# Silu on ScalarE in the FFN, and long-lived tiles in one SBUF tile: a two-layer SSD and HGRN2 trunk on one core

## The chip, the core and the metric

The kernel runs on one core of one Trainium2 chip. A core has a matrix engine (TensorE, PE in the profile; PEld is its weight load), three vector-like engines (VectorE, DVE; ScalarE, ACT; GpSimd, POOL) and SyncE (SP), whose queue issues all transfers of this kernel. The metric is the device time of one execution in microseconds. Each engine works through its own instructions in order and waits on semaphores for the others.

## The reference

One inference step of a small encoder for a prompt of 1024 frames and a running stream of 32 frames, in float32. Two layers: a Mamba-2 SSD mixer and then an HGRN2 mixer, each followed by a SwiGLU FFN, with RMS norms before them and one at the end. The part that the first half of the change touches is

```
def swiglu(h, w_gate, w_up, w_down):
    return (jax.nn.silu(h @ w_gate) * (h @ w_up)) @ w_down
...
x = x + swiglu(rmsnorm(x, ffn_norm_w[layer]), ffn_w_gate[layer], ffn_w_up[layer], ffn_w_down[layer])
```

with D_MODEL 1024 and a hidden width of 2816. The mixers keep running states (SSD: 32 heads of 64 x 128; HGRN2: 8 heads of 128 x 128), which are outputs too, as is the last part of the convolution's input.

## The kernel before

The frames lie along the free dimension, the features along the 128 partitions: the residual x is 8 tiles `acc` for each of two halves, of 512 and of 544 frames (512 of the prompt and the 32 of the stream). Every float32 product is made of three float32r products: an operand is split into a high part (a ScalarE Copy that rounds) and a low part (a VectorE subtraction), and TensorE adds high x high, low x high and high x low (`product`, L275; lines 282 to 284).

The FFN's hidden width is cut into 11 slabs of 256. The first slabs of a half (two of half 0, one of half 1) are the head: `ffn_up` (L995) makes gate and up products tile by tile, and runs between the last pieces of the mixer. The other slabs go through `ffn_unit` (L921), a seven-product scheme (Strassen-Winograd) on 2 x 2 blocks: a unit makes 256 output features of gate or of up from one 1024 x 256 slab of weights, in seven `part`s of 12 matmuls each (L917 to 919). Its weights are loaded by `unit_raw` (L873) as two tiles of 1024 columns, and `unit_weights` (L888) makes the seven combinations from them on VectorE (with a scratch tile `s1`) and splits each (`hl`) into one of the six `ws` buffers. `unit_raw` counts units in `NU`: an odd unit loads both its tiles into `Y`, which has one buffer; an even one takes two of the three buffers of the ring `raw`. Units come in pairs, a gate unit and then an up unit, so before the change the gate units are the odd ones.

A unit is a generator with five steps (one `part` in the first, two in the second and the third, one in the fourth and the fifth). `in_turn` (L957) lays the units over each other: up[1], gate[4], up[2], gate[5], then up[3], next gate[1], up[4], next gate[2], up[5], next gate[3], and so on. At the end of a gate unit stands its `after` (L978): tanh on ScalarE, then (tanh + 1) x gate by a scalar_tensor_tensor on VectorE; the factor 0.5 comes in `ffn_upper` (L986), where gate is multiplied by up and the result is split into `fh` and `fl`. Down products of the group of slabs before (`ffn_outs`, L1039; four weight tiles through the ring `raw`, split by `wsplit`) run at the end of the first gate unit of a group, that is after gate[5] and before up[3]; a group has two slabs, in some places one. After the second group's, `x_stat` (L832) takes the next norm's statistics (`rkeep`: squares, a Ln and an Exp on ScalarE).

Tiles come from pools: a tile of a tag waits until one of the tag's buffers is free (counts in `BUFS`, L43). Their addresses in SBUF, those of the PSUM banks, and the order in which each engine issues are worked out by a planner before the launch, from the order as written, the priorities (`lifted`) and its own estimate of times; tiles of different tags may share addresses at different times. `small` (L72) gives 128-column scratch tiles of tag `s`, five buffers for all of their uses. The SSD states `Sst` and the HGRN2 states `Sh` share the four tiles of tag `st`.

Of the kernel before, what the change touches and what calls it, by code (L numbers as in the profile page):

```python
# [16 lines left out]
P = 128  # L17
# [24 lines left out]
TW = 552  # L42
BUFS = {"xn": 16, "x": 12, "ys": 8, "cb": 4, "xd": 2, "ec": 1, "ss": 1, "xr": 2, "n": 4, "w": 3, "s": 5}  # L43
WIDTH = {k: 512 if k == "xr" else TW if k in ("x", "w") else LEN[1] for k in BUFS}


@with_exitstack
def trunk_kernel(ctx, tc, x_prompt, x_sample, state_ssd, cache_conv, state_hgrn,
# [22 lines left out]

    def small(s, w=P, dt=F32):  # L72
        return sp.tile([P, w], dt, tag="s", bufs=BUFS["s"], name=nm(s))

# [40 lines left out]

    ident = cp.tile([P, P], F32, name="ident")
    make_identity(nc, ident)
    ones = cp.tile([P, P], F32, name="ones")
    V.memset(ones, 1.0)
    epsc = cp.tile([P, 1], F32, name="epsc")  # L120
    V.memset(epsc, EPS)
    lss = cp.tile([P, 13], F32, name="lss")
    epst = lss[:, 12:13]
    mhalf = cp.tile([P, 8], F32, name="mhalf")
    G.memset(mhalf, -0.5)
    cmask = cp.tile([P, P], F32, name="cmask")
# [4 lines left out]
    rmask = cp.tile([P, LEN[1]], F32, name="rmask")  # L131
    V.memset(rmask, 1.0)
# [3 lines left out]
    for i in range(2):  # L136
        t = cp.tile([P, P], F32, name=f"scz{i}")
        V.memset(t, 0.0)
        scz.append(t)


    acc = [[cp.tile([P, LEN[h]], F32, name=f"acc{h}_{m}") for m in range(KD)] for h in range(2)]

    xss = cp.tile([P, 2, 9], F32, name="xss")
    xr = cp.tile([P, 9], F32, name="xr")

# [36 lines left out]

    vc = cp.tile([P, NVC], F32, name="vc")
    cw = cp.tile([P, 96], F32, name="cw")
    cc = cp.tile([P, 72], F32, name="cc")
    dtb = cp.tile([P, 1], F32, name="dtb")
    acol = cp.tile([P, 1], F32, name="acol")
    dcol = cp.tile([P, 16], F32, name="dcol")
    lbt = cp.tile([P, 6, 8], F32, name="lbt")  # L190
    c1, c0, nc1 = lbt[:, 3, :], lbt[:, 4, :], lbt[:, 5, :]
# [68 lines left out]
    def wraw(parts, kt):  # L260
        raw = wp.tile([P, 1024], F32, tag="raw", bufs=3, name=nm("raw"))
        r3 = raw.rearrange("p (k c) -> p k c", k=kt)
        for (lo, hi, src) in parts:
            dma(r3[:, :, lo:hi], src.rearrange("(k p) c -> p k c", p=P))
        return raw

    @lifted("wl")
    def wsplit(raw, kt):
        wh = wp.tile([P, 1024], F32R, tag="ws", bufs=6, name=nm("wh"))
        wl = wp.tile([P, 1024], F32R, tag="ws", bufs=6, name=nm("wl"))  # L270
# [32 lines left out]

    XN = ["xn"] * 16
    XN2 = ["x"] * 12 + ["cb"] * 4
# [15 lines left out]
    @lifted("norm")  # L321
    def norm(h, wc, out, tags, blocks=None, r=None):

        for (b0, bn) in blocks or ((0, LEN[h]),):
            mmb = BLK[h] if blocks is None else [(0, bn)]
            if r is None:
                r = rstd_of([acc[h][m][:, b0:b0 + bn] for m in range(KD)], mmb, 1.0 / D, bn)
            for m in range(KD):
                xf = T("n", "xf")
                stt(xf[:, :bn], acc[h][m][:, b0:b0 + bn], vc[:, wc + m:wc + m + 1], r[:, :bn], MUL, MUL)  # L330
                if m == len(out):
                    out.append((T(tags[2 * m], "h", F32R), T(tags[2 * m + 1], "l", F32R)))
# [9 lines left out]

    carry = cp.tile([P, NCT, 3], F32, name="carry")
    newc = cp.tile([P, 2, 3, NCT], F32, name="newc")
    Sst = [cp.tile([P, 512], F32, tag="st", bufs=NG, name=f"Sst{g}") for g in range(NG)]
    cumd = [dp.tile([32, LEN[h]], F32, name=f"cumd{h}") for h in range(2)]
# [4 lines left out]
    def ssd_dt(h, xn, blocks):  # L351
# [33 lines left out]
        act(pk[96:128, :L], cum[96:128, :L], AF.Exp)  # L385
        lastc = cp.tile([P, 5], F32, name=f"lastc{h}")
        V.tensor_copy(lastc[96:128, :4], pk[96:128, P - 1:H1:P])
# [4 lines left out]
        dma(lastd[h][:, :nch], lastc[96:128, :nch])  # L392
        elast = cp.tile([P, 32, 5], F32, tag="elast", bufs=2, name=f"elast{h}")
        dma(elast[:, :, :nch], lastd[h][:, :nch].unsqueeze(0).to_broadcast([P, 32, nch]))
        return pk, None, elast

    def ssd_cols(h):
        pk, _, elast = dts[h]
        cols = cp.tile([P, 5, P], F32, tag="cols", bufs=1, name=f"cols{h}")
# [174 lines left out]
    def ssd_layer(after, w0):  # L574
# [16 lines left out]
        for i, (h, g) in enumerate(units):  # L591
# [14 lines left out]
            if g == 0:  # L606
                ssd_cols(h)
            Yt = sp.tile([P, 4 * LEN[1]], F32, tag="Y", bufs=1, name=nm("Y"))
            u["Y"] = Yt.rearrange("p (j t) -> p j t", j=4)
            Ss = None  # L610
            if h:
                Ss = T("ss", "Ss")[:, :512]
                sr = T("xr", "sr")
                dma(sr.rearrange("p (j n) -> p j n", n=P),
# [33 lines left out]

    Shb = [cp.tile([P, 512], F32, tag="st", bufs=NG, name=f"Sh{i}") for i in range(2)]
    Sh = [Shb[e // 4][:, (e % 4) * P:(e % 4 + 1) * P] for e in range(8)]  # L650
# [136 lines left out]
    def hgrn_layer(after):  # L787
# [4 lines left out]
        for i, (h, e) in enumerate(units):  # L792
# [16 lines left out]
            if e % 2 == 0:  # L809
                yt = sp.tile([P, 4 * LEN[1]], F32R, tag="Y", bufs=1, name=nm("hy"))  # L810
                yp = yt.rearrange("p (j t) -> p j t", j=4)
# [19 lines left out]

    def x_stat(h, tag):  # L832

        keep = T(tag, "rkeep")
        return rstd_of([acc[h][m][:, :LEN[h]] for m in range(KD)], BLK[h], 1.0 / D, LEN[h], keep)

    def norm_pieces(h, wc, out, blocks, r):

        def piece(m, b0, bn):
            xf = T("n", "xf")  # L840
            stt(xf[:, :bn], acc[h][m][:, b0:b0 + bn], vc[:, wc + m:wc + m + 1], r[:, b0:b0 + bn], MUL, MUL)
            if m == len(out):
                out.append((T("xn", "h", F32R), T("xn", "l", F32R)))
            xh, xl = out[m]
# [28 lines left out]
    def unit_raw(src):  # L873

        NU[0] += 1
        if NU[0] % 2:
            t = sp.tile([P, 4 * LEN[1]], F32, tag="Y", bufs=1, name=nm("raw2"))
            halves = [t[:, q * 1024:(q + 1) * 1024] for q in range(2)]
        else:
            halves = [wp.tile([P, 1024], F32, tag="raw", bufs=3, name=nm("raw")) for _ in range(2)]  # L880
        out = []
# [6 lines left out]
    def unit_weights(src):  # L888
# [3 lines left out]
        def hl(x):  # L892
            w = wp.tile([P, 1024], F32R, tag="ws", bufs=6, name=nm("wh"))
# [81 lines left out]
    def ffn_gate(layer, h, s, xn, tx, g):  # L975
        L = LEN[h]

        def after(dst):  # L978
            g.extend(dst)
            for x in g:  # L980
                t = T("w", "ft")
                act(t[:, :L], x[:, :L], AF.Tanh, scale=0.5)
                stt(x[:, :L], t[:, :L], 1.0, x[:, :L], ADD, MUL)
        return ffn_unit(h, ffn_w_gate[layer][:, s * 256:(s + 1) * 256], xn, tx, "w", after)

    def ffn_upper(layer, h, s, xn, tx, g, hid):  # L986
        L = LEN[h]

        def after(dst):
            for x, y in zip(g, dst):  # L990
                stt(y[:, :L], x[:, :L], 0.5, y[:, :L], MUL, MUL)
                hid.append(split(y[:, :L], L, (T("ys", "fh", F32R), T("ys", "fl", F32R))))
        return ffn_unit(h, ffn_w_up[layer][:, s * 256:(s + 1) * 256], xn, tx, "xd", after)

    def ffn_up(layer, h, s, i, hid, xn):  # L995
# [6 lines left out]
        for (b0, bn) in BLK[h]:  # L1002
# [99 lines left out]
    def mixer_ffn(mixer, layer, wc, nxt):  # L1102
# [15 lines left out]
        r = []  # L1118
        due = ffn_half(layer, 1, xn[1], tx[1], 1, lambda: r.append(nxt and x_stat(0, "ss")),
                       [2] if nxt else [1, 1])  # L1120
# [70 lines left out]
    for q in range(2):  # L1191
        wrow.append(T(("ec", "ss")[q], "wrow")[:, :512])
        dma(wrow[q], final_norm_w[q * 512:(q + 1) * 512].unsqueeze(0).to_broadcast([P, 512]))
# [38 lines left out]
```

## Time and profile before

| | |
|---|---|
| time, median of 3 runs | 2942.97 us (2942.57 to 2947.24) |
| profiled execution, its own time | 2942.06 us |
| its span (first to last instruction) | 2940.3 us |
| mean granted TensorE clock | 0.994 |
| moved from and to HBM | 272.39 MB read, 7.82 MB written |

The profile is of one execution. Busy time is the time in which an engine had an instruction in work; matmuls are pipelined, and their ends are modelled, so that a busy TensorE isn't TensorE at its peak. Rows of groups give an engine, an operation, out<-in with the program's names, how many, and then the busy time in us and the mean of one in ns, and behind a bar the engine's idle time just before them and what ended most of it. Rows of waits give who waited for whom, the total in us, how often, and the longest. Because most helpers make their instructions on one line (L86 for ScalarE, L89 and L92 for VectorE, L98 for transfers), groups are told apart by the names of the tiles: `ft` is the FFN's tanh, `fw` the gate, `fxd` up and then the hidden value, `wh` and `wl` the split weights, `raw` any weight tile as loaded.

### The profile page before, as it was taken

The numbers are of one execution on the slowest core, as the hardware profiler recorded it, in microseconds if no ns is written. First come the engines' busy times: TensorE is split into PE (matmuls) and PEld (weight loads), VectorE is DVE, ScalarE is ACT, GpSimd is POOL, SyncE is SP. The second block draws the span as 40 slices with busy tenths as digits, with TensorE's granted clock in tenths as the row PEclk, the third lists the DMA queues.
The fourth block names the chain that finished last, engine by engine and source line by source line (L and its number), as shares of the span: only waits on it lengthen the run. The fifth ranks groups of instructions, "written<-read, shape, count | busy, mean of one in ns | idle before, by whom it ended". The sixth has DMA issues, their size and how long they took to land.

```text
span 2940.3 us, 49353 instructions
## 1 busy us (share of the span) xinstructions
PE 2855.9 (97%) x19655; PEld 2618.4 (89%) x19655; DVE 2205.6 (75%) x3879; ACT 1551.3 (53%) x2944; POOL 52.7 (2%) x156
## 2 busy tenths in 40 slices
PE   7999999999999999999999999999999999999998
PEld 6777788989988999899999888899988999999997
DVE  6877787877887987897777555655578977887777
ACT  6745545554643654455544555655554644454445
POOL 0000001000100000000000000000000000000000
PEclk9999999999999999999999999999999999999999
DMA  5443424343333333322333222222222333323332
GB/s 146 123 111 94 108 76 122 106 113 98 109 80 105 98 98 108 108 80 87 101 94 99 79 79 80 69 76 76 78 84 87 108 96 99 111 87 94 94 94 103
DMA packets 401346, 283.42 MB, mean 96 GB/s; under 512 B 28873, under 2 KB 386778, under 8 KB 401114
## 3 DMA queue, kind: packets, MB, share of 16 engines
q1 hardware_dynamic: 401114, 280.25, 32.7%
q8 instruction: 154, 2.52, 0.4%
q14 instruction: 78, 0.64, 0.1%
HBM read 272.39 MB, written 7.82 MB: 95 GB/s over the span
## 4 chain that ended last, share of the span: by engine, by line
PE 75%; DVE 12%; DMA 6%; ACT 5%; issue 2%; SPq 0%; DVEq 0%; POOL 0%; ACTq 0%; POOLq 0%
PE mm L282 16%; PE mm L284 16%; PE mm L283 16%; PE mm L919 3%; PE mm L917 3%; PE mm L918 3%; PE sc L919 3%; PE sc L917 3%; PE sc L918 3%; DMA cumB<-cumd 3%; DMA raw<-in_ffn_w_gate_dram 2%; DVE wh L89 2%; ACT wh L86 1%; PE sc L509 1%; ACT cumB L86 1%
## 5 line engine op out<-in xcount | busy, mean ns | idle before, releaser
L86 ACT ACTIVATE wh<-raw 128x512 fp32r<-128x512 f32 (+1 forms) x688 | 554.2, 817 | 592.4 <-PE mm L283 363.3
L282 PE MATMUL mm<-h,wh 128*128 128x272 f32 (+2 forms) x2064 | 675.0, 328 | 7.9 <-ACT h L86 3.9
L284 PE MATMUL mm<-h,wl 128*128 128x272 f32 (+2 forms) x2064 | 668.5, 324 | 2.7 <-DVE wl L89 2.7
L283 PE MATMUL mm<-l,wh 128*128 128x272 f32 (+2 forms) x2064 | 668.3, 324 | 1.3 <-DVE l L89 0.9
L89 DVE TENSOR_TENSOR wl<-raw,wh 128x1024 fp32r<-128x1024 f32 x308 | 376.0, 1222 | 150.7 <-ACT wh L86 149.3
L282 PEld LDWEIGHTS mm<-h,wh 128*128 128x128 f32 x2064 | 390.0, 189 | 38.1 <-ACT h L86 4.9
L284 PEld LDWEIGHTS mm<-h,wl 128*128 128x128 f32 x2064 | 390.2, 189 | 33.0 <-DVE wl L89 3.9
L283 PEld LDWEIGHTS mm<-l,wh 128*128 128x128 f32 x2064 | 390.4, 189 | 30.9 <-DVE l L89 3.1
L282 PE MATMUL mm<-fh,wh 128*128 128x272 f32 (+1 forms) x1056 | 343.2, 326 | 8.9 <-DVE fxd L89 7.8
L283 PE MATMUL mm<-fl,wh 128*128 128x272 f32 (+1 forms) x1056 | 342.2, 325 | 1.8 <-DVE fl L89 1.8
L89 DVE TENSOR_TENSOR acc<-mm,acc 128x272 f32<-128x272 f32 (+1 forms) x512 | 259.6, 524 | 110.3 <-PE mm L284 107.6
L284 PE MATMUL mm<-fh,wl 128*128 128x272 f32 (+1 forms) x1056 | 341.1, 324 | 0.6 <-DVE wl L89 0.6
L89 DVE TENSOR_TENSOR wh<-raw,wh 128x512 fp32r<-128x512 f32 x380 | 258.2, 688 | 20.6 <-ACT wh L86 17.7
L917 PE MATMUL mm<-th,wh 128*128 128x272 f32 (+1 forms) x912 | 260.9, 286 | 0.4 <-ACT s L86 0.4
L919 PE MATMUL mm<-th,wh 128*128 128x272 f32 (+1 forms) x912 | 259.6, 285 | 0.2 <-DVE wh L89 0.2
L918 PE MATMUL mm<-tl,wh 128*128 128x272 f32 (+1 forms) x912 | 259.6, 285 | 0.0
L282 PEld LDWEIGHTS mm<-fh,wh 128*128 128x128 f32 x1056 | 198.8, 189 | 26.9 <-DVE fxd L89 9.3
L283 PEld LDWEIGHTS mm<-fl,wh 128*128 128x128 f32 x1056 | 199.6, 189 | 17.7 <-DVE fl L89 3.4
L284 PEld LDWEIGHTS mm<-fh,wl 128*128 128x128 f32 x1056 | 199.5, 189 | 16.1 <-DVE wl L89 1.0
L917 PE MATMUL sc<-h,wh 128*128 128x272 f32 (+1 forms) x608 | 173.7, 286 | 0.5 <-ACT wh L86 0.5
L917 PEld LDWEIGHTS mm<-th,wh 128*128 128x128 f32 x912 | 171.7, 188 | 2.5 <-ACT s L86 1.7
L919 PE MATMUL sc<-h,wh 128*128 128x272 f32 (+1 forms) x608 | 173.3, 285 | 0.0
(261 smaller groups left out, 5961.0 us busy)
## 6 DMA issues: line engine op xcount, KB each, us to landing
raw<-in_ffn_w_down_dram SPq DMA_DIRECT2D x90, 512.0 KB, 3.5
raw<-in_ffn_w_gate_dram SPq DMA_DIRECT2D x88, 512.0 KB, 4.9
raw<-in_ffn_w_up_dram SPq DMA_DIRECT2D x88, 512.0 KB, 3.8
raw<-in_ssd_in_w_dram SPq DMA_DIRECT2D x80, 512.0 KB, 4.6
raw<-in_hgrn_in_w_dram SPq DMA_DIRECT2D x64, 512.0 KB, 4.1
cumB<-cumd SPq DMA_DIRECT2D x64, 256.0 KB, 4.1
raw<-in_ssd_out_w_dram SPq DMA_DIRECT2D x32, 512.0 KB, 3.7
raw<-in_hgrn_out_w_dram SPq DMA_DIRECT2D x16, 512.0 KB, 3.2
```

The source lines that it names most:

```text
L86: A.activation(out=out, in_=in_, func=f, **kw)
L89: (eng or V).tensor_tensor(out=out, in0=a, in1=b, op=op)
L282: PE.matmul(ps[:, :bn], a, mh, start=(k == 0), stop=False)
L283: PE.matmul(ps[:, :bn], a, ml, start=False, stop=False)
L284: PE.matmul(ps[:, :bn], b, mh, start=False, stop=(k == n - 1))
L509: PE.matmul(pp, Btok[:n, :], xw[:n, :], start=True, stop=True)
L917: PE.matmul(ps[:, :n], a, mh, start=(k == 0 and not more), stop=False, skip_group_check=True)
L918: PE.matmul(ps[:, :n], a, ml, start=False, stop=False, skip_group_check=True)
L919: PE.matmul(ps[:, :n], b, mh, start=False, stop=(k == 3), skip_group_check=True)
```

## The change

Two things. In the FFN, silu is made by ScalarE's Silu, in place on the gate tile (in the head from PSUM into `ft`), and the product with up is a plain tensor_tensor. And tiles that live long, or whose rotation is simple, are laid into one tile `fixed` of 14368 columns by `place` (which rounds each up to 16 columns), or, for the normed input, into one tile `xn` of 16 slots; what stays in pools has widths of TW (552) columns or two or four times that. The small scratch tiles become rings written out by hand. `s1` and the kept statistics move into the four `st` tiles, and `NU` is raised in `unit_weights`, after `unit_raw` has read it.

```diff
+FIXED = 14368
-BUFS = {"xn": 16, "x": 12, "ys": 8, "cb": 4, "xd": 2, "ec": 1, "ss": 1, "xr": 2, "n": 4, "w": 3, "s": 5}
-WIDTH = {k: 512 if k == "xr" else TW if k in ("x", "w") else LEN[1] for k in BUFS}
+BUFS = {"x": 12, "ys": 8, "cb": 4, "xd": 2, "ec": 1, "ss": 1, "xr": 2, "n": 4, "w": 3}
+WIDTH = {k: TW for k in BUFS}
...
-    def small(s, w=P, dt=F32):
-        return sp.tile([P, w], dt, tag="s", bufs=BUFS["s"], name=nm(s))
+    def slot(tag, s):
+        return T(tag, s, F32R) if isinstance(tag, str) else tag
+
+    rings = {"diag": (0, 2), "cbm": (2, 2), "Btok": (4, 2), "hT": (0, 2), "hSp": (2, 4), "fss": (4, 2), "nco": (0, 1)}
+    at = {}
+
+    def small(s, w=P):
+
+        at[s] = at.get(s, -1) + 1
+        if s == "hec":
+            return hec[at[s] % 3][:, :w]
+        first, n = rings[s]
+        return smalls[first + at[s] % n][:, :w]
...
+    fixed = cp.tile([P, FIXED], F32, name="fixed")
+    used = [0]
+
+    def place(w):
+        used[0] += -(-w // 16) * 16
+        return fixed[:, used[0] - -(-w // 16) * 16:][:, :w]
+
+    smalls, hec = [place(P) for _ in range(6)], [place(16) for _ in range(3)]
...
-    acc = [[cp.tile([P, LEN[h]], F32, name=f"acc{h}_{m}") for m in range(KD)] for h in range(2)]
+    acc = [[place(LEN[h]) for m in range(KD)] for h in range(2)]
...
-        raw = wp.tile([P, 1024], F32, tag="raw", bufs=3, name=nm("raw"))
+        raw = wp.tile([P, 2 * TW], F32, tag="raw", bufs=3, name=nm("raw"))[:, :1024]
...
-    XN = ["xn"] * 16
+    colt = place(5 * P)
+    xnt = cp.tile([P, 16, LEN[1]], F32R, name="xn")
+    XN = [xnt[:, i] for i in range(16)]
...
-    Sst = [cp.tile([P, 512], F32, tag="st", bufs=NG, name=f"Sst{g}") for g in range(NG)]
+    st = [place(TW) for _ in range(NG)]
+    Sst = [t[:, :512] for t in st]
...
     def unit_raw(src):
 
-        NU[0] += 1
         if NU[0] % 2:
-            t = sp.tile([P, 4 * LEN[1]], F32, tag="Y", bufs=1, name=nm("raw2"))
+            t = sp.tile([P, 4 * TW], F32, tag="Y", bufs=1, name=nm("raw2"))
...
-        s1 = T("xr", "s1")[:, :512].rearrange("p (k c) -> p k c", k=4)
+        NU[0] += 1
+        s1 = st[NU[0] % 2][:, :512].rearrange("p (k c) -> p k c", k=4)
...
             for x in g:
-                t = T("w", "ft")
-                act(t[:, :L], x[:, :L], AF.Tanh, scale=0.5)
-                stt(x[:, :L], t[:, :L], 1.0, x[:, :L], ADD, MUL)
+                act(x[:, :L], x[:, :L], AF.Silu)
...
             for x, y in zip(g, dst):
-                stt(y[:, :L], x[:, :L], 0.5, y[:, :L], MUL, MUL)
+                tt(y[:, :L], x[:, :L], y[:, :L], MUL)
...
             t = T("w", "ft")
-            act(t[:, :bn], pg[:, :bn], AF.Tanh, scale=0.5)
-            stt(t[:, :bn], t[:, :bn], 1.0, pg[:, :bn], ADD, MUL)
-            stt(t[:, :bn], t[:, :bn], 0.5, pu[:, :bn], MUL, MUL)
+            act(t[:, :bn], pg[:, :bn], AF.Silu)
+            tt(t[:, :bn], t[:, :bn], pu[:, :bn], MUL)
...
-        due = ffn_half(layer, 0, xn[0], tx[0], HEAD, lambda: r.append(x_stat(1, "ec")), [2])
+        due = ffn_half(layer, 0, xn[0], tx[0], HEAD, lambda: r.append(x_stat(1, st[2])), [2])
```

The other vectors, masks and states (`ident`, `vc`, `carry`, `lastc`, `elast` and so on) go through `place` in the same way, and the rows of the last norm's weight (`wrow`) lie in `st[2]` and `st[3]`.

More of the change, by code (lines that the diff above doesn't have):

```diff
@@ L130, in trunk_kernel @@
     umask = cmask.bitcast(U32)
-    rmask = cp.tile([P, LEN[1]], F32, name="rmask")
+    rmask = place(LEN[1])
     V.memset(rmask, 1.0)
@@ L136, in trunk_kernel @@
     for i in range(2):
-        t = cp.tile([P, P], F32, name=f"scz{i}")
+        t = place(P)
         V.memset(t, 0.0)
         scz.append(t)
-    acc = [[cp.tile([P, LEN[h]], F32, name=f"acc{h}_{m}") for m in range(KD)] for h in range(2)]
-    xss = cp.tile([P, 2, 9], F32, name="xss")
-    xr = cp.tile([P, 9], F32, name="xr")
+    acc = [[place(LEN[h]) for m in range(KD)] for h in range(2)]
+    xss = place(2 * 9).rearrange("p (a b) -> p a b", b=9)
+    xr = place(9)
     def x_rows(h, c):
@@ L182, in over_partitions @@
             PE.matmul(out[:, c * P:c * P + n], ones[:n, :], d[:n, :n], start=True, stop=True)
[L184 to L190, printed above, removed]
+    vc = place(NVC)
+    cw = place(96)
+    cc = place(72)
+    dtb = place(1)
+    acol = place(1)
+    dcol = place(16)
+    lbt = place(6 * 8).rearrange("p (a b) -> p a b", b=8)
     c1, c0, nc1 = lbt[:, 3, :], lbt[:, 4, :], lbt[:, 5, :]
@@ L268, in wsplit @@
     def wsplit(raw, kt):
-        wh = wp.tile([P, 1024], F32R, tag="ws", bufs=6, name=nm("wh"))
-        wl = wp.tile([P, 1024], F32R, tag="ws", bufs=6, name=nm("wl"))
+        wh = wp.tile([P, 2 * TW], F32R, tag="ws", bufs=6, name=nm("wh"))[:, :1024]
+        wl = wp.tile([P, 2 * TW], F32R, tag="ws", bufs=6, name=nm("wl"))[:, :1024]
         act(wh, raw, AF.Copy)
@@ L331, in norm @@
                 if m == len(out):
-                    out.append((T(tags[2 * m], "h", F32R), T(tags[2 * m + 1], "l", F32R)))
+                    out.append((slot(tags[2 * m], "h"), slot(tags[2 * m + 1], "l")))
                 xh, xl = out[m]
@@ L385, in ssd_dt @@
         act(pk[96:128, :L], cum[96:128, :L], AF.Exp)
-        lastc = cp.tile([P, 5], F32, name=f"lastc{h}")
+        lastc = place(5)
         V.tensor_copy(lastc[96:128, :4], pk[96:128, P - 1:H1:P])
@@ L392, in ssd_dt @@
         dma(lastd[h][:, :nch], lastc[96:128, :nch])
-        elast = cp.tile([P, 32, 5], F32, tag="elast", bufs=2, name=f"elast{h}")
+        elast = place(160).rearrange("p (h c) -> p h c", c=5)
         dma(elast[:, :, :nch], lastd[h][:, :nch].unsqueeze(0).to_broadcast([P, 32, nch]))
@@ L398, in ssd_cols @@
         pk, _, elast = dts[h]
-        cols = cp.tile([P, 5, P], F32, tag="cols", bufs=1, name=f"cols{h}")
+        cols = colt[:, :5 * P].rearrange("p (c t) -> p c t", t=P)
         for c, (o, n, _) in enumerate(CHUNKS[h]):
@@ L607, in ssd_layer @@
                 ssd_cols(h)
-            Yt = sp.tile([P, 4 * LEN[1]], F32, tag="Y", bufs=1, name=nm("Y"))
+            Yt = sp.tile([P, 4 * TW], F32, tag="Y", bufs=1, name=nm("Y"))[:, :4 * LEN[1]]
             u["Y"] = Yt.rearrange("p (j t) -> p j t", j=4)
@@ L646, in half_two_dt @@
         dts[1] = ssd_dt(1, xns[1], BLK[1])
-    Shb = [cp.tile([P, 512], F32, tag="st", bufs=NG, name=f"Sh{i}") for i in range(2)]
+    Shb = [t[:, :512] for t in st[:2]]
     Sh = [Shb[e // 4][:, (e % 4) * P:(e % 4 + 1) * P] for e in range(8)]
@@ L809, in hgrn_layer @@
             if e % 2 == 0:
-                yt = sp.tile([P, 4 * LEN[1]], F32R, tag="Y", bufs=1, name=nm("hy"))
+                yt = sp.tile([P, 4 * TW], F32R, tag="Y", bufs=1, name=nm("hy"))[:, :4 * LEN[1]]
                 yp = yt.rearrange("p (j t) -> p j t", j=4)
@@ L830, in trunk_kernel, with x_stat @@
     NB = 1
-    def x_stat(h, tag):
-        keep = T(tag, "rkeep")
+    def x_stat(h, keep):
         return rstd_of([acc[h][m][:, :LEN[h]] for m in range(KD)], BLK[h], 1.0 / D, LEN[h], keep)
@@ L842, in piece @@
             if m == len(out):
-                out.append((T("xn", "h", F32R), T("xn", "l", F32R)))
+                out.append((XN[2 * m], XN[2 * m + 1]))
             xh, xl = out[m]
@@ L873, in unit_raw @@
     def unit_raw(src):
-        NU[0] += 1
         if NU[0] % 2:
-            t = sp.tile([P, 4 * LEN[1]], F32, tag="Y", bufs=1, name=nm("raw2"))
+            t = sp.tile([P, 4 * TW], F32, tag="Y", bufs=1, name=nm("raw2"))
             halves = [t[:, q * 1024:(q + 1) * 1024] for q in range(2)]
         else:
-            halves = [wp.tile([P, 1024], F32, tag="raw", bufs=3, name=nm("raw")) for _ in range(2)]
+            halves = [wp.tile([P, 2 * TW], F32, tag="raw", bufs=3, name=nm("raw"))[:, :1024] for _ in range(2)]
         out = []
@@ L892, in hl @@
         def hl(x):
-            w = wp.tile([P, 1024], F32R, tag="ws", bufs=6, name=nm("wh"))
+            w = wp.tile([P, 2 * TW], F32R, tag="ws", bufs=6, name=nm("wh"))[:, :1024]
             v = w.rearrange("p (q k c) -> p q k c", q=2, k=4)
@@ L1118, in mixer_ffn @@
         r = []
-        due = ffn_half(layer, 1, xn[1], tx[1], 1, lambda: r.append(nxt and x_stat(0, "ss")),
+        due = ffn_half(layer, 1, xn[1], tx[1], 1, lambda: r.append(nxt and x_stat(0, st[3])),
                        [2] if nxt else [1, 1])
```

20 lines of the change are left out of this document (10 added, 10 removed).

## The prediction

> **What bounds the kernel now.** I read the page first (busy time, then the chain that ended last), then stretches of each stage, then who waits for whom.
>
> ```profile
> span 2940.3 us, 49353 instructions
> PE 2855.9 (97%) x19655; PEld 2618.4 (89%) x19655; DVE 2205.6 (75%) x3879; ACT 1551.3 (53%) x2944; POOL 52.7 (2%) x156
> PE 75%; DVE 12%; DMA 6%; ACT 5%; issue 2%; SPq 0%; DVEq 0%; POOL 0%; ACTq 0%; POOLq 0%
> PE mm L282 16%; PE mm L284 16%; PE mm L283 16%; PE mm L919 3%; PE mm L917 3%; PE mm L918 3%; PE sc L919 3%; PE sc L917 3%; PE sc L918 3%; DMA cumB<-cumd 3%; DMA raw<-in_ffn_w_gate_dram 2%; DVE wh L89 2%; ACT wh L86 1%; PE sc L509 1%; ACT cumB L86 1%
> ...
> 240.00:300.00 60.00, 56.59 (x281) 44.89 (x279) 39.65 (x57) 24.66 (x46) 2.33 (x8) 1.00 0.39 110
> 1320.00:1380.00 60.00, 57.90 (x446) 57.19 (x445) 46.52 (x82) 33.08 (x60) 0.00 (x0) 0.97 0.27 81
> 1380.00:1440.00 60.00, 60.00 (x480) 59.81 (x479) 45.69 (x81) 27.53 (x52) 0.00 (x0) 1.00 0.33 105
> 1680.00:1740.00 60.00, 60.00 (x290) 48.65 (x289) 33.22 (x63) 33.21 (x52) 0.00 (x0) 1.00 0.27 79
> ```
>
> A row of a stretch is: its length, then busy time of PE, PEld, DVE, ACT and POOL, the granted clock, the DMA share and GB/s. TensorE is the bound. It is busy 2855.9 of 2940.3 us, so everything else together leaves it 84.4 us of idle time, 2.9%: no edit off TensorE can win more than that and the clock lost after such waits. The FFN (about 960 to 1620 us and 2240 to 2900 us; 1380 to 1440 is a full stretch of it) runs at 60.00 of 60 while VectorE is at 46 and ScalarE at 28 of 60. The Silu edit takes work from VectorE in just this stage, where it has 14 us of every 60 to spare; only what makes TensorE wait counts. The chain has two transfers in it, cumB in the SSD layer (untouched here) and, in the FFN, the gate weights.
>
> Who TensorE waits for (total us, times, longest):
>
> ```profile
> PE sc L509 <- DVE xw L89: 8.9, 10, 1.4
> PE mm L282 <- DVE fxd L89: 7.8, 7, 2.1
> ...
> PE sc L748 <- ACT hkv L86: 0.9, 1, 0.9
> ```
>
> The first is inside an SSD chunk, which the change leaves as it is. The second belongs to the FFN. One of its seven, from the timelines of VectorE, SyncE's queue and TensorE, with the clock behind it:
>
> ```profile
> 1328.61 0.69 DVE L89 TENSOR_TENSOR wh<-raw,wh 128x512 fp32r<-128x512 f32 x1
> ...
> 1334.89 0.69 DVE L89 TENSOR_TENSOR s<-raw 128x512 f32<-128x512 f32 x1 [2.51 <-DMA raw<-in_ffn_w_gate_dram]
> 1335.50 0.68 DVE L89 TENSOR_TENSOR sq<-sq,sq 128x512 f32<-128x512 f32 x1
> 1336.10 0.44 DVE L89 TENSOR_TENSOR fxd<-sc,s 128x272 f32<-128x272 f32 x1
> ...
> 1329.33 0.92 SPq L98 DMA_DIRECT2D raw<-in_ffn_w_gate_dram  x2
> ...
> 1336.59 0.40 PE L282 MATMUL mm<-fh,wh 128*128 128x272 f32 x1 [2.10 <-DVE fxd L89]
> ...
> 1338.00:1341.00 3.00, 3.00 (x15) 3.00 (x14) 2.64 (x4) 1.41 (x4) 0.00 (x0) 0.50 0.26 65
> 1341.00:1344.00 3.00, 3.00 (x25) 3.00 (x25) 2.08 (x4) 1.85 (x3) 0.00 (x0) 0.96 0.33 115
> ...
> 1470.93 0.69 DVE L89 TENSOR_TENSOR s<-raw 128x512 f32<-128x512 f32 x1 [2.07 <-DMA raw<-in_ffn_w_gate_dram]
> ...
> 1472.03 0.39 PE L282 MATMUL mm<-fh,wh 128*128 128x272 f32 x1 [0.41 <-DVE fxd L89]
> ```
>
> Gate units load their weights into Y, which has one buffer. The last split that reads the old gate weights starts at 1328.61, the new load is issued at 1329.33, and VectorE stands 2.51 us in front of `s<-raw`, the sum that needs it. Queued behind it on VectorE is `fxd<-sc,s`, the read that frees the PSUM bank that the down product wants, so TensorE stands 2.10 us. A wait of 2.07 us cost TensorE only 0.41: some 1.7 us are absorbed. After the long wait the granted clock is 0.50 for 3 us: 15 matmuls start there, 25 in the next 3 us, so 10 are lost, 10 x 0.12 = 1.2 us more. This was the only stretch of those that I read where the clock fell behind such a wait.
>
> **The change part by part.**
>
> ```profile
> L86 ACT ACTIVATE ft<-fw 128x544 f32<-128x544 f32 x40 | 26.1, 653 | 0.3
> L86 ACT ACTIVATE ft<-fw 128x512 f32<-128x512 f32 x36 | 22.6, 628 | 0.4
> L92 DVE SCALAR_TENSOR_TENSOR fw<-ft,fw 128x544 f32<-128x544 f32 x40 | 28.9, 721 | 1.1
> L92 DVE SCALAR_TENSOR_TENSOR fw<-ft,fw 128x512 f32<-128x512 f32 x36 | 24.8, 688 | 0.2
> L92 DVE SCALAR_TENSOR_TENSOR fxd<-fw,fxd 128x512 f32<-128x512 f32 x36 | 24.8, 690 | 0.0
> L89 DVE TENSOR_TENSOR fl<-fxd,fh 128x512 fp32r<-128x512 f32 x36 | 24.9, 692 | 0.6
> L92 DVE SCALAR_TENSOR_TENSOR ft<-ft,mm 128x512 f32<-128x512 f32 x16 | 11.0, 686 | 11.2 <-PE mm L284 8.2 <-ACT ft L86 3.0
> L92 DVE SCALAR_TENSOR_TENSOR ft<-ft,mm 128x272 f32<-128x272 f32 x16 | 7.0, 435 | 9.4 <-ACT ft L86 4.8 <-PE mm L284 4.6
> L86 ACT ACT_TABLE_LOAD x96 | 123.2, 1283 | 17.8 <-DVE hec L687 8.2 <-DVE hlg L89 7.2 <-PEq L1219 0.8
> ```
>
> *Silu.* Gate units: 40 + 36 Tanh become as many Silu over the same elements; no Silu is in this trace, the nearest row is the Tanh that it replaces, so I take equal (0). The 76 scalar_tensor_tensor that made silu go: 28.9 + 24.8 = 53.7 us of VectorE. In the heads (`ffn_up`) half of the two groups `ft<-ft,mm` goes, (11.0 + 7.0) / 2 = 9.0 us. The product with up turns from a scalar_tensor_tensor (690 ns at 512) into a tensor_tensor (692): 0. VectorE loses 62.7 us, all beside a TensorE at 60 of 60. Value on the end: 0, bounds 0 and -3.
>
> *Table loads.* The trace has 96, each 1.28 us, in front of Ln, Exp, Tanh and Sqrt groups; FFN Tanh needs none of its own after an Exp. Silu, if it lies apart from Exp, needs one wherever the FFN's activations resume after an Exp. By ScalarE's order that is seven times: twice in each layer's head, once after each of the three statistics (`rkeep`). 7 x 1.28 = 9.0 us of ScalarE, and what hides it is that ScalarE is at 28 of 60. The nearest thing on the path is the 0.9 us that TensorE waited once for `hkv` in the HGRN head. I take +1, bounds 0 and +9. The Trainium skill, "ScalarE: Activation LUTs", section "What ACT_TABLE_LOAD costs", speaks against such a change: a switch costs about 2.66 us with its drain. By that figure the seven would be 18.6 us of ScalarE; the trace's 96 loads have 123.2 us busy and 17.8 us of idle time in front of all of them, which bears out the load and shows little of a drain.
>
> *Weights.* `NU` is now raised after `unit_raw` reads it, so its parity turns: gate units load into two of the three `raw` buffers, up units into Y. The rows of the waits on both sides:
>
> ```profile
> DVE s L89 <- DMA raw<-in_ffn_w_gate_dram: 32.8, 16, 3.5
> DVE s L89 <- DMA raw<-in_ffn_w_up_dram: 24.0, 17, 2.7
> ...
> ACT wh L86 <- DMA raw<-in_ffn_w_down_dram: 149.6, 41, 5.0
> ACT wh L86 <- DMA raw<-in_ffn_w_gate_dram: 20.4, 19, 1.9
> ...
> raw<-in_ffn_w_gate_dram SPq DMA_DIRECT2D x88, 512.0 KB, 4.9
> ```
>
> Where down products run, the up unit held two `raw` buffers, so four down tiles went through the third one by one: ScalarE's 41 waits of 3.6 us. They had cover (the six split buffers hold the next parts). Now the gate's two are free by then, down tiles use three, and the next gate load comes behind them with a whole set of down products to land in (two slabs, 544 columns: 192 matmuls at 60 / 480 = 0.125 us, 24 us). So the seven waits go: -7.8, and -1.2 of clock. What is late next: the up load into Y, which is issued when the last up unit's last split is done and is wanted three parts (36 matmuls, 36 x 0.125 = 4.5 us) later, against the 4.9 us that a gate load took to land (the last row, from the page's transfers). VectorE or ScalarE will wait in front of it some 0.3 to 2 us at each of 38 up units; queued behind `s<-raw` there is the next gate unit's `fw<-sc,s`, whose bank TensorE wants. Gate loads with no down products between had the same distance, and TensorE shows no wait at them. I take +1, bounds 0 and +19 (below).
>
> *Places.* `fixed` and `xn` hold what was in tiles of their own; the work, its order as written and the counts of x, ys, cb, n, w are the same, `xn` slots are overwritten in the same sequence, and the small rings have nine places for the five of tag `s`. Waits for memory in the trace are those of rings that stay (raw, cumB). Value 0; a changed allocation also reshuffles the order in which the planner issues, which I bound by the largest stall it could make or remove in the layers, the 8.9 us of `xw`, to either side.
>
> Sum: -7.8 - 1.2 + 0 + 1 + 1 + 0 = -7.0 us on the profiled execution, 2942.06 us (span 2940.3 and 1.8 around it): 2935.1. The median of the runs, 2942.97, is 0.9 above that execution: **2936.0**.
>
> **Rivals.**
> 1. *The stall only moves.* The gate's load now queues behind down loads that wait for splits, so VectorE stands in front of the same `s<-raw`, and +9 comes back. For it: every one of these tiles goes through SyncE's one queue in order. Against: the down products give it some 24 us, of which it needs 4.9. Time 2943 (within +-4).
> 2. *Slower: Y under the up units.* 38 turnarounds in place of the 16 that hurt. If each costs TensorE what the 16 gate waits cost it, 7.8 / 16 = 0.49 us, that is 38 x 0.49 = 18.6, with the 9.0 won and 1 of tables: 2943 - 9.0 + 1 + 18.6 = 2953.6. It decides from where the wait passes the 1.7 us that are absorbed. Against it: gate loads at that distance were late by about 1.1 us (20.4 / 19).
> 3. *More: less VectorE in front of TensorE.* If the freed 62.7 us and the new order also took half of the waits on `xw` and the few on `sq`, `wl`, `fl`: a further 10, 2926.
> 4. *Tables at every pair.* If Silu's table did not hold Copy, 38 + 16 Silu groups would load twice: 54 x 2 x 1.28 = 139 us of ScalarE, still under its idle time, with TensorE hit as above by about 0.5 each: 2943 + 27 = 2970. Against it: Copy, Square and Relu cost no load anywhere beside Tanh, Exp or Ln in this trace. The same page, section "Table sets: the hidden batching unit", says that copy, relu and identity lie in every set; by that rule this rival is out.
>
> **How the numbers follow.** Forecast 0.45 (2931 to 2940), rival 1 0.28, rival 2 0.14, rival 3 0.10, rival 4 0.03. About 0.2% (5.9 us) is what a measurement of this kernel can tell from no change: faster means below 2937.1, slower above 2948.9. Of the forecast some two thirds lie below 2937.1 (0.30), with rival 3 (0.10) and a little of rival 1 (0.02): faster 0.42. Slower: rivals 2 and 4 less their lower ends, and the reshuffle's upper end: 0.17. Same: 0.41. The range reaches from rival 3 to rival 2: 2924 to 2954; the forecast's own is 2931 to 2940.
>
> **What would show it.** After: no TensorE wait on `fxd` of 1 to 2 us where down products begin; ScalarE's waits for down weights well under 149.6; VectorE waits for gate weights near 0 and those for up weights at up to 38 places, below 1.7 us each; 103 table loads; Silu at 653 and 628 ns; VectorE near 2143 us. I am wrong if TensorE waits at the up units (rival 2), if table loads pass 110 (rival 4), or if the difference lies before 900 us or between 1620 and 2240, where only the reshuffled order could have made it.

## The result, and the profile after

| | before | after |
|---|---|---|
| time, median on the same chip | 2946.41 us (2942.57 to 2949.01, 5 runs) | 2895.88 us (2894.16 to 2896.89, 5 runs) |
| ratio, 95% interval | | 0.9831 [0.9816, 0.9845] |
| span of the profiled execution | 2940.3 us | 2894.0 us |

The changed kernel is faster by 1.7%, well below the range of the prediction. The page of the kernel after, first its span and then the busy time of the engines:

```profile
span 2894.0 us, 49037 instructions
...
PE 2843.8 (98%) x19655; PEld 2615.4 (90%) x19655; DVE 2158.1 (75%) x3787; ACT 1563.9 (54%) x2951; POOL 43.2 (1%) x156
```

The work is the same on TensorE (19655 matmuls), its idle time fell from 84.4 us to 2894.0 - 2843.8 = 50.2 us, and its busy time by 12.1 us. To see where, I take the start of the instructions that add a product to the residual (`acc<-mm,acc` before, `fixed<-mm,fixed` after, 512 in both), counted from 0, and compare the same one in both traces (after less before, us):

```
number and place in the program         before    after    difference
 80  end of the SSD layer                892.6    863.5     -29.1
256  behind the first FFN               1765.0   1728.4     -36.6
352  end of the HGRN2 layer             2250.6   2212.9     -37.7
496  end of the second FFN              2906.9   2862.5     -44.4
```

So 29 us come from the SSD layer, where not a line of the arithmetic changed, 7.5 from the first FFN and the residual around it, 6.7 from the second, 1 from HGRN2. Between the same places TensorE starts the same number of matmuls in both traces. Up to the 80th accumulation its idle time falls from 48.8 to 27.1 us and its busy time from 843.8 to 836.4; from the 80th to the 256th the idle time falls from 10.1 to 4.7, from the 352nd to the 496th from 6.9 to 2.5. The prediction had looked for everything in the FFN.

**The SSD layer.** Stretches before (length, then busy PE, PEld, DVE, ACT, POOL, clock, DMA share, GB/s; in brackets the instructions that start):

```profile
100.00:380.00 280.00, 267.25 (x1330) 208.82 (x1329) 213.35 (x312) 152.46 (x281) 12.99 (x37) 1.00 0.40 107
380.00:520.00 140.00, 132.76 (x890) 116.17 (x889) 112.45 (x173) 73.99 (x159) 10.25 (x24) 0.98 0.38 102
```

and after:

```profile
100.00:380.00 280.00, 279.60 (x1411) 220.66 (x1410) 223.84 (x327) 162.79 (x302) 10.79 (x37) 1.00 0.40 109
380.00:520.00 140.00, 135.29 (x983) 120.12 (x982) 117.01 (x188) 74.61 (x164) 6.73 (x24) 1.00 0.43 113
```

In the first stretch TensorE stood 12.75 of 280 us before and 0.40 after, at the same granted clock. What it stood for is best read in the chain of work. The chain before, in order of time, between 490 and 530 us (start, length, what; SPq is the queue of SyncE; shorter pieces left out):

```profile
492.25 0.61 PE sc L520 x8
492.88 0.37 SPq L98
493.35 4.61 DMA cumB<-cumd
498.04 0.16 ACT cumB L86
498.20 0.15 issue
498.35 1.49 ACT cumB L86 x4
499.84 0.95 ACT wh L86
500.79 0.29 ACT z L86
501.17 0.29 issue
501.45 0.69 DVE xw L89
502.15 0.14 issue
502.29 1.10 PE sc L509 x2
503.38 0.61 PE sc L520 x8
504.01 3.87 DMA cumB<-cumd
507.96 0.84 ACT cumB L86 x3
```

This is a loop, once per chunk. The product `sc<-cumB,xdt` (L520) of one chunk reads a `cumB` tile for the last time; the load of a later chunk's `cumB` goes into that same place, so SyncE's queue lets it go only then; it takes 4.61 us to land; ScalarE, which works in order, stands in front of the Relu that reads it, and behind that Relu stand a weight split and a `z` that have nothing to do with it; VectorE's `xw` comes after those, and TensorE's next product (L509) after `xw`. From one L520 to the next are 11.1 us, and of them 5 are queue and transfer. The waits in the SSD layer (100 to 900 us) say the same. Before, ScalarE and SyncE's queue:

```profile
ACT cumB L86 <- DMA cumB<-cumd: 75.4, 35, 6.2
...
SPq L98 <- DVE cumB L89: 141.4, 32, 13.4
SPq L98 <- PE sc L520: 93.6, 32, 6.1
```

After:

```profile
ACT cumB L98 <- DMA cumB<-cumd: 3.0, 8, 0.6
...
SPq L110 <- ACT cumB L98: 4.4, 3, 1.6
...
SPq L110 <- PE sc L544: 0.4, 1, 0.4
```

The queue no longer waits for the product (L544 is the old L520) nor for VectorE's last pass over `cumB`, and ScalarE's 75.4 us are 3.0. Why can the load go earlier, when the ring has four buffers as before? The built programs tell: the count of a ring orders the work, but the waits come from the addresses that the planner gave.

```
                 cumB tiles  places  of these behind  median us from a load's
                                     another cumB     issue to its first Relu
before               72         4        68               4.4
after                72        29         7               9.7
```

In the kernel after, the tile that `cumB` replaces is in 65 of 72 cases one of another tag, and one that has been done with for some time. (That all pool tiles have one width now is the likely reason; no run changed the widths alone.) The load is issued some 5 us earlier, and the loop is open: the 29 us are 0.8 us for each of the 36 chunks. It isn't more because TensorE's own work is the next bound (140.00 of 140 us between 520 and 660 after).

**The FFN.** The same views after, waits first, then the stretch from 1320 to 1380 us, which the prediction showed for the kernel before (the kernel after is some 30 us further on in its program there):

```profile
DVE fixed L101 <- DMA raw<-in_ffn_w_gate_dram: 31.8, 23, 2.7
...
ACT wh L98 <- DMA raw<-in_ffn_w_up_dram: 28.5, 33, 1.8
...
ACT wh L98 <- DMA raw<-in_ffn_w_down_dram: 8.2, 5, 2.1
```

```profile
1320.00:1380.00 60.00, 59.91 (x472) 59.09 (x471) 43.18 (x75) 34.73 (x63) 0.00 (x0) 1.00 0.32 97
```

ScalarE's 149.6 us in front of down weights are 8.2, the wait of TensorE for `fxd` is gone from the list, and 472 matmuls start where 446 did, at a clock of 1.00 for 0.97. Silu and the table loads:

```profile
L98 ACT ACT_TABLE_LOAD x103 | 132.1, 1283 | 18.3 <-DVE fixed L711 15.8 <-PEq L1239 0.8
L98 ACT ACTIVATE fw<-fw 128x544 f32<-128x544 f32 x40 | 26.3, 657 | 7.4 <-DVE fw L101 6.6
L98 ACT ACTIVATE fw<-fw 128x512 f32<-128x512 f32 x36 | 22.6, 627 | 3.9 <-DVE fw L101 3.6
```

### The profile page after: what moved, and what is told of

Same layout as the page of the kernel before. It is cut to its first block, busy times and chain, and to the rows that moved or that the text cites. A ratio compares the mean times of both kernels' runs of the same rounds, so it can differ in the third digit from the quotient of the medians.

```text
span 2894.0 us, 49037 instructions
## 1 busy us (share of the span) xinstructions
PE 2843.8 (98%) x19655; PEld 2615.4 (90%) x19655; DVE 2158.1 (75%) x3787; ACT 1563.9 (54%) x2951; POOL 43.2 (1%) x156
## 5 line engine op out<-in xcount | busy, mean ns | idle before, releaser
L303 PE MATMUL mm<-xn,wh 128*128 128x272 f32 (+2 forms) x1552 | 524.2, 338 | 1.7 <-ACT xn L98 1.3
L304 PE MATMUL mm<-xn,wh 128*128 128x272 f32 (+2 forms) x1552 | 519.0, 335 | 1.2 <-DVE xn L101 1.2
L305 PE MATMUL mm<-xn,wl 128*128 128x272 f32 (+2 forms) x1552 | 518.0, 334 | 1.2 <-DVE wl L101 1.2
L101 DVE TENSOR_TENSOR wl<-raw,wh 128x1024 fp32r<-128x1024 f32 x308 | 375.5, 1221 | 75.4 <-ACT wh L98 57.4
L101 DVE TENSOR_TENSOR fixed<-mm,fixed 128x272 f32<-128x272 f32 (+1 forms) x512 | 262.5, 523 | 194.4 <-PE mm L305 192.8
L303 PEld LDWEIGHTS mm<-xn,wh 128*128 128x128 f32 x1552 | 292.9, 189 | 32.1 <-issue 2.8
L305 PEld LDWEIGHTS mm<-xn,wl 128*128 128x128 f32 x1552 | 292.9, 189 | 31.1 <-issue 2.0
L304 PEld LDWEIGHTS mm<-xn,wh 128*128 128x128 f32 x1552 | 292.5, 188 | 29.3 <-DVE xn L101 1.7
L941 PE MATMUL sc<-xn,wh 128*128 128x272 f32 (+1 forms) x608 | 173.1, 285 | 0.0
L942 PE MATMUL sc<-xn,wh 128*128 128x272 f32 (+1 forms) x608 | 172.8, 284 | 0.0
```

Of the source, the lines that this page charges most:

```text
L101: (eng or V).tensor_tensor(out=out, in0=a, in1=b, op=op)
L303: PE.matmul(ps[:, :bn], a, mh, start=(k == 0), stop=False)
L304: PE.matmul(ps[:, :bn], a, ml, start=False, stop=False)
L305: PE.matmul(ps[:, :bn], b, mh, start=False, stop=(k == n - 1))
L941: PE.matmul(ps[:, :n], a, ml, start=False, stop=False, skip_group_check=True)
L942: PE.matmul(ps[:, :n], b, mh, start=False, stop=(k == 3), skip_group_check=True)
```

## The experiments

Two theories stood against each other for the 29 us: (A) the loop through `cumB`'s transfer, (B) the places of all the other tiles (`ec` had one place before and 14 after, `cth` one and 24, `xdt` and `xw` two each and over 20), with Silu and the weights' turn as parts of their own. All ratios are against the kernel before on the same chip. The last columns compare the 80th and the 496th accumulation of one trace with those in the trace of before, from a chip on which that kernel's median was 2946.41 us; on those of the experiments it was 2936 to 2938. The kernels that were traced more than once (after and after_again, place_only and place_only_again) differ by 0.9 and 1.6 us at the 80th and by 2.5 and 1.1 at the 496th, so two or three us in these columns say nothing.

```
run                        ratio   95% interval       at 80   at 496
silu_only                  1.0038  [1.0023, 1.0053]    +2.4    +4.0
place_only                 0.9854  [0.9839, 0.9869]   -29.8   -47.1
parity_only                0.9979  [0.997, 0.9989]     +5.3    -9.4
parity_undone              1.0019  [1.0009, 1.0028]    -2.5    -0.8
cumb_four                  0.9936  [0.992, 0.9953]     -2.5   -19.8
cumb_six                   0.9964  [0.9951, 0.9977]    +0.9   -15.1
cumb_eight                 0.9938  [0.9923, 0.9953]    -5.3   -21.8
raw_three                  0.984   [0.9825, 0.9855]   -30.3   -48.8
cumb_four_544              0.9937  [0.992, 0.9953]     +2.4   -16.8
two_rings_four             0.9856  [0.9842, 0.9871]   -27.3   -46.9
parity_undone_load_ring    0.9953  [0.9938, 0.9968]   -16.1   -12.5
after_load_ring            0.9853  [0.9838, 0.9868]   -27.0   -43.7
parity_undone_load_four    0.99    [0.9886, 0.9913]   -25.7   -31.2
after_again                0.9849  [0.9836, 0.9863]   -30.0   -46.9
place_only_again           0.9849  [0.9836, 0.9862]   -31.4   -48.2
tanh_raw_three             0.9844  [0.9831, 0.9858]   -31.4   -50.7
```

### Silu alone, and everything but Silu

`silu_only` is the kernel before with the FFN's three Silu edits of the diff; `place_only` is the kernel after with tanh and scalar_tensor_tensor put back.

> The kernel before with the three Silu edits alone; tiles and NU as before. Theory A (places: a tile may lie at any free address, so its load needn't wait for the tile of its own tag) : no gain, ratio 0.998 to 1.002, PE still waits some 17 us on L509 in the SSD layer and some 8 us on fxd in the FFN. Theory B (VectorE's relief): a third or more of the 47 us, ratio below 0.995, mostly in the FFN. 103 table loads in either.

> The changed kernel with tanh and the two scalar_tensor_tensor put back; places, widths, rings and NU as changed. Theory A: nearly the whole gain, ratio 0.982 to 0.986. Theory B: a ratio of 0.988 or more, the FFN slower than in the changed kernel by 10 us or more. 96 table loads.

Silu alone won nothing and cost 0.4%; everything but Silu has the whole gain. Where the 0.4% lies the traces don't tell: silu_only's is 2.4 us late at the end of the SSD layer, before any Silu has run, and 4.0 in the end, not much more than two traces of one kernel differ by.

### The weights' turn alone, and its undoing

```diff
-        if NU[0] % 2:
+        if not NU[0] % 2:
```

`parity_only` has this line in the kernel before (gate units load into `raw`, up units into `Y`), `parity_undone` has it in the kernel after.

> The kernel before with the parity of NU turned alone: gate units load into raw, up units into Y. Theory C (the parity takes the gate load off the turnaround of Y): the waits on fxd at the start of the down products go, -7 to -10 us, ratio 0.9965 to 0.998, all of it after 960 us. Theory A alone (the parity does nothing while three raw addresses serve all loads): within 0.2%. My recorded rival 2 (Y under the up units) would show PE waits at the up units and a ratio over 1.002.

> The changed kernel with the parity of NU as before: gate units in Y. The planner gives other addresses to it as well: 13 for the 72 cumB tiles and 3 for raw, where the changed kernel has 29 and 7 and the kernel before 4 and 3. Theory A alone: the SSD gain stays for the most part (end of the SSD layer's last accumulation 20 to 29 us earlier than before), the FFN gain shrinks. Theory C: the FFN loses its 13 us, ratio to before about 0.988. If all came from Silu or the order: ratio as changed, 0.983.

The waits of parity_only in the FFN:

```profile
ACT wh L86 <- DMA raw<-in_ffn_w_up_dram: 26.7, 32, 2.1
...
DVE s L89 <- DMA raw<-in_ffn_w_gate_dram: 21.2, 16, 2.7
ACT wh L86 <- DMA raw<-in_ffn_w_down_dram: 12.7, 11, 2.1
```

That is the FFN of the kernel after, in the kernel before: no TensorE wait for `fxd` is left, and from the 80th to the 496th accumulation 14.7 us are won, 5.3 of them given back in the SSD layer in front. parity_undone was the surprise: its weights are turned back, which has nothing to do with the SSD layer, and the gain is gone there too. Its waits in that layer:

```profile
ACT cumB L98 <- DMA cumB<-cumd: 82.5, 36, 7.5
```

In its program 58 of 72 `cumB` tiles stand again behind a `cumB` (median 4.35 us from issue to Relu), with the same widths and the same `fixed`. So `fixed`, the small rings and the equal widths don't open the loop by themselves; the places that came out of the planner do, and a one-word edit elsewhere changes them. But `ec` is back in one place too here, so this run doesn't tell (A) from (B).

### cumB in a ring of its own, raw in a ring of its own

In the kernel after, `cumB` goes by hand through a ring of 4, 6 or 8 places, or `raw` through one of 3:

```diff
+    cbr = cp.tile([P, 4, TW], F32, name="cbr")
+    cbn = [0]
+
+    def cb_slot():
+        cbn[0] += 1
+        return cbr[:, cbn[0] % 4, :512]
...
-            cb = T("cb", "cumB")[:, :512].rearrange("p (h t) -> p h t", t=P)
+            cb = cb_slot().rearrange("p (h t) -> p h t", t=P)
```

> The changed kernel with cumB in a ring of four places of its own, as tag cb nominally is. The planner then also gives raw three places (380 of 384 raw tiles follow a raw tile). Theory A1 (the SSD gain is the turnaround of cumB: with four places the load of chunk c+1 waits for the last reader of chunk c-1): the last accumulation before the SSD layer's end (the 64th) is at most 5 us earlier than before, not 28; SyncE's queue waits again some 90 us on L544 and ScalarE some 75 us on cumB; ratio 0.995 to 0.999, what is left being the FFN's. Theory A2 (the order or the small rings make the SSD gain): the 64th accumulation stays 20 us or more earlier, ratio 0.986 to 0.989.

> The same with six places of 512 columns for cumB. Theory A1: a load may run a chunk further ahead, so most of the SSD gain is back, the 64th accumulation 20 to 28 us earlier than before, ratio 0.987 to 0.991, ScalarE's waits on cumB below 25 us. Theory A2: no difference to the ring of four beyond 0.2%.

> The same with eight places. Theory A1: like six or up to 5 us better, ScalarE waits on cumB below 10 us; if six is already enough, the same within 0.2%. Theory A2: as the ring of four.

> The changed kernel with raw in a ring of three places of its own; cumB stays free (12 of 72 follow another cumB). Theory A1: the SSD layer as in the changed kernel, the 64th accumulation 25 to 30 us earlier than before. For the FFN two ways: if the parity alone made its 13 us (gate loads off Y), ratio 0.982 to 0.985; if the wider choice of places for raw did, the FFN gives back 5 us or more, ratio 0.986 to 0.988.

raw_three keeps the whole gain, so `raw`'s seven places (three before) have no part in it. With four places for `cumB` the SSD layer's gain is gone, as (A) says; but six and eight did not bring it back, which I had taken for a test of (A). cumb_eight's waits in the SSD layer:

```profile
ACT cbr L105 <- DMA cbr<-cumd: 75.0, 37, 5.6
...
SPq L117 <- PE sc L551: 84.1, 28, 5.7
```

A load still waits for the product, one four chunks back now. With a bigger ring the planner moves the Relus forward by as much: one of cumb_eight's loads is issued at 107.2 us, right behind the product that ends at 107.1, ScalarE's Relu reads it at 111.2, and its own product comes only at 179. From a Relu to the product that reads its tile the median is 20.6 us with four places, 49.4 with six and 91.5 with eight; from a load's issue to its Relu it stays at 4.3, 4.4 and 4.6. These rings are always full, and so give the transfer no time, however long they are. The three runs also gave the other tiles other places: cumb_four put `ec` back in one, so it loses what (B) needs as well; cumb_six and cumb_eight have `ec` in 18 and 14 places, `cth` in 20 and 17, and are at +0.9 and -5.3 us at the 80th accumulation all the same, which speaks against (B).

### One factor at a time

A place 544 columns wide in place of 552 (`cumb_four_544`) leaves `cumB` tight and gives the other tiles about as many places as in the kernel after (`ec` 21, `cth` 24, `xdt` 20, `xw` 17). `two_rings_four` goes the other way: cumb_four, but the load goes into a ring of its own, and Relu writes the tight ring:

```diff
+    ldr = cp.tile([P, 4, 512], F32, name="ldr")
...
-            cb = cb_slot().rearrange("p (h t) -> p h t", t=P)
+            cb = ld_slot().rearrange("p (h t) -> p h t", t=P)
...
+            ld3 = cums[q]
+            cb3 = cb_slot().rearrange("p (h t) -> p h t", t=P)
+            cums[q] = cb3
...
-                act(cb3[:n, i, :n], cb3[:n, i, :n], AF.Relu, scale=-1.0, bias=cols[:n, c, hh:hh + 1])
+                act(cb3[:n, i, :n], ld3[:n, i, :n], AF.Relu, scale=-1.0, bias=cols[:n, c, hh:hh + 1])
```

> The changed kernel with cumB in a ring of its own of four places, as in cumb_four, only that a place is 544 wide instead of 552. In the built program every other tile then gets as many places as in the changed kernel (ec 21, cth 24, raw 8), where cumb_four gave ec one place and raw three of its own turn. So it holds cumB alone tight. Theory A, it is cumB's transfer behind the product that frees its place: ScalarE's wait for cumB is back (70 to 100 us in the SSD layer), the SSD layer loses its gain (the 64th accumulation within 6 us of before, not 28 earlier), 0.990 to 0.997 of the time before. Rival B, it is the places of all the other tiles (ec, cth, xdt, xw, raw): the 64th accumulation is 20 to 30 us earlier than before, whatever ScalarE waits for cumB, 0.980 to 0.986.

> cumb_four with the load taken out of cumB's ring: the transfer goes into one of four places of its own, Relu reads it there and writes the ring of four. A load then waits only for an earlier Relu, and Relu waits for the product that frees its place with no transfer between them. Theory A: ScalarE's wait for the loaded tile falls from 88 us to under 25, and the SSD gain comes back (64th accumulation 20 to 30 us earlier than before), 0.981 to 0.988 of the time before. Rival B (other tiles' places): the wait goes, the time stays within 5 us of cumb_four, 0.992 to 0.996. Beside A: raw and ec are less bound here than in cumb_four, so a gain alone says less than cumb_four_544 beside it.

cumb_four_544, waits of the SSD layer and then its first stretch:

```profile
ACT cbr L105 <- DMA cbr<-cumd: 113.3, 42, 8.9
...
PE sc L540 <- DVE xw L108: 11.8, 10, 2.6
```

```profile
100.00:380.00 280.00, 266.92 (x1337) 208.57 (x1335) 210.80 (x305) 150.93 (x278) 10.72 (x37) 1.00 0.39 104
```

two_rings_four, the same:

```profile
ACT cbr L112 <- PE sc L560: 97.4, 33, 5.7
...
PE sc L549 <- DVE xw L115: 1.1, 1, 1.1
```

```profile
100.00:380.00 280.00, 278.77 (x1407) 219.89 (x1406) 223.56 (x326) 162.95 (x301) 11.74 (x37) 1.00 0.40 108
```

With places in plenty for everything else and `cumB` tight, nothing is won in the SSD layer (+2.4 at the 80th accumulation); with the transfer out of the loop, 27.3 of the 29.1 us are back. So places in plenty don't make the gain without the transfer out of the loop: as a cause by itself (B) falls, and (A) stands. One combination was not run: in two_rings_four `ec` has 15 places and `cth` 21, and in the other runs with the gain they have as many or about so (14 to 21 and 21 to 24). Whether the open loop would win as much with all other tiles as tight as before is not shown.

Look at ScalarE's own wait: 97.4 us in two_rings_four, more than the 87.7 us that it waited for the transfer in cumb_four. The sum of a wait is no measure of its price: here ScalarE is ahead of TensorE and waits for its product (L560 is the old L520), in cumb_four it is behind and TensorE waits in the end.

### The load ring in other kernels

`after_load_ring` and `parity_undone_load_ring` have a load ring of two places, `parity_undone_load_four` one of four. With two places the next chunk's load takes the place ahead of the current chunk's Relu, which so reads the next chunk's decays and waits for the later load; they do not compute what the reference does, and their times are read with that in mind.

> The changed kernel with cumB's load in two places of its own, read by Relu there. Theory A: nothing is left to win, since the wait for cumB is gone already: 0.981 to 0.986 of the time before, the same as the changed kernel. Rival: two places for the load are too few, each load waits for the Relu of the chunk before, and part of the wait is back: 0.987 to 0.995.

> parity_undone (the changed kernel with the weights' halves turned back; 1.002 of the time before) with cumB's load in two places of its own, read by Relu there. Weights as before, raw on three places of its own turn (381 of 384 follow a raw). Theory A: the SSD layer gains 20 to 30 us against before and the two FFN layers gain nothing, ScalarE still waits 150 us or so for the down weights; 0.990 to 0.994 of the time before. Rival B: like parity_undone, 0.999 to 1.003.

> parity_undone (the changed kernel with the weights' halves as before, 1.002 of the time before) with cumB's load in four places of its own, so that the load of the next chunk does not take the place that the current chunk still reads. If the SSD layer's gain comes from the transfer of cumB alone: the 64th accumulation 20 to 30 us earlier than before, no further gain in the two FFN layers, ScalarE's wait for the down weights still 130 us or more, 0.988 to 0.993 of the time before. If the gain needs the turned weights too: 0.997 or more.

In the kernel after, where the loop is open already, nothing more is to be had (0.9853). With the weights turned back (parity_undone), a load ring of four places brings the end of the SSD layer 25.7 us ahead of before, and the time falls from 1.0019 to 0.99. So the gain of the SSD layer doesn't need the weights' turn; it needs the transfer out of the loop. Two things came out otherwise than expected: ScalarE's wait for down weights is 100.9 us, not 130 or more, and from the 80th to the 496th accumulation this run takes 7.2 us less than parity_undone, though it was to win nothing there (`raw` has five places in it, three in parity_undone). The ring of two, with its later load, gets 16.1 us and a ratio of 0.9953, between what the two theories gave.

### Silu's price again, and the best of the parts

> The changed kernel itself, on the same chip as the next one. 0.981 to 0.986 of the time before.

> The changed kernel with tanh and scalar_tensor_tensor in the FFN, for the price of Silu. In the kernel before, Silu alone cost 0.4%. If that is Silu's own price (table loads, ScalarE busier in front of the up products), this is 0.003 to 0.005 below after_again; if it was the order that the edit shuffled there, it is within 0.002 of after_again, on either side.

> place_only with the raw weights in three places of their own turn, the two edits that did not cost anything apart: as a candidate to beat both kernels. If the two add up, 0.978 to 0.983 and below after_again by 0.003 or more; if the differences of raw_three and place_only from the changed kernel were only the chip's spread, within 0.002 of after_again.

On one chip the kernel after takes 2892.48 us, with tanh 2892.75, with tanh and `raw` in three places 2891.07: the same. Silu has no price and no gain that shows here, and no version beats the kernel after by a difference that these intervals can tell. What made silu_only's 0.4% in the kernel before stays open.

## Why the prediction was wrong

It gave 2936.0 us, 0.9976 of the 2942.97 us that it started from; measured is 0.9831.

*Places*, valued at 0, is the step that failed. It said "Waits for memory in the trace are those of rings that stay (raw, cumB)": the ring stayed in the text, its places did not, 4 and then 29. In the first part it had put the same aside: "The chain has two transfers in it, cumB in the SSD layer (untouched here)". That row, "DMA cumB<-cumd 3%", was the sign: some 88 us of transfers on the chain of a stage in which TensorE stood 12.75 of 280 us. The bound for a reshuffle was wrong too. It took one row, TensorE's 8.9 us on `xw`. But the loop ends at one instruction, L509, and its waits go by the name of what came last: `xw` 8.9, `wh` 5.5 and `Btok` 2.3 are 16.7 us. All of TensorE's named waits from 100 to 790 us add up to 25.1 us, which is the idle time of the stretches there (25.3). Measured: -29.1 us, of which 21.8 are idle time; the other 7.3 lie in the busy time of the same 5545 matmuls (the granted clock between 380 and 520 us, 0.98 before and 1.00 after, is some 2.8 of them; the rest is open). The fact that was needed stands in the description of the kernel before, that tiles of different tags may share addresses; what the change does to that was not asked.

The prediction named its own refutation, "if the difference lies before 900 us": that is where two thirds of it are.

*Weights*: the mechanism held, the size was off. The term was -7.8 - 1.2 + 1 = -8 us; parity_only's two FFNs gave 14.7, the kernel after's 7.5 + 6.7 = 14.2. The seven waits on `fxd` are gone, but their 7.8 us were not all: in the two FFN parts (80th to 256th and 352nd to 496th accumulation) TensorE's idle time falls from 17.0 us before to 6.5 in parity_only, and its busy time by 4.2 for the same matmuls, where the term had 1.2 for the clock. ScalarE's waits on down weights (149.6 to 8.2), which the term counted at nothing because six split buffers cover them, went too. A hint that they do cost something is parity_undone_load_four: against parity_undone the waits on `fxd` stay (8.9 us, and 8.2 in parity_undone), those on down weights fall from 159.2 to 100.9, and the 7.2 us above are won. No run took them apart. The wait on up weights is where it was put, 33 places, 1.8 us at most, on ScalarE, and TensorE doesn't feel it: rival 2 is out. VectorE's wait for gate weights, said to go to near 0, stayed (32.8 to 31.8 us). Before, seven of these waits ended 1.1 to 1.7 us ahead of a set of down products, and these are the seven that TensorE felt; after, 16 of 23 lie inside a set that is already running, and the nearest of the others is 4.9 us ahead of one. So rival 1 was right that VectorE would still stand there, and wrong that TensorE would feel it.

*Silu*: 0, and 0 measured in the kernel after (2892.48 against 2892.75); 657 and 627 ns for 653 and 628 forecast; VectorE 2158.1 us for 2143. Silu takes 49.5 us of VectorE's busy time (2207.6 in place_only), not the 62.7 that the rows of its instructions add up to. *Table loads*: 103 as forecast, so rival 4 is out, 8.9 us more of ScalarE for 9.0, and no price in the time. By the Trainium skill, "ScalarE: Activation LUTs", section "What ACT_TABLE_LOAD costs" (2.66 us a switch with its drain), the estimate for the seven is 18.6 us; the trace has 1.283 us a load and 18.3 us of idle time in front of all 103, where it was 17.8 for 96, so it shows the load and not the drain. *Rival 3* alone lay on the right side of the forecast, at 2926, and its reason was in part luck: it halved the waits on `xw` by VectorE's relief and the new order. They fell from 8.9 to 1.5 us, but in place_only as well, where VectorE has as much to do as before.

## What to carry to other kernels

A transfer on the chain of waits whose queue waits for a product, and whose reader feeds the next product, is a loop: price it by all of TensorE's waits in its stage, whatever their names, and by the stretches' idle time, not by the largest row. Give such a load a place that is free long before it is needed (here a landing buffer of four tiles, emptied by the first reader, did it), since a longer ring in which the order runs ahead by as much has no slack either. Where a planner chooses addresses, an edit in one stage can change waits in another: look at which tile each loaded tile replaces.

## What the runs showed that was not expected

- A one-word edit in the FFN (parity_undone) and 8 columns of one ring's width (cumb_four and cumb_four_544) gave most tiles other places. The first took the SSD layer's gain back (-2.5 us at the 80th accumulation, for -29.1); the second changed nothing (0.9936 and 0.9937): `cumB` was tight in both. What in the planner decides between such layouts was not pursued.
- A 256 KB load of `cumB`, which spreads rows over all partitions, takes 4.1 us in the median from issue to landing before and 5.0 after. It is slower in the faster kernel, and it doesn't matter there.
